# A two-layer hybrid decoder: the final norm moved into the last loop, new places for the hooked parts, and 18 matmuls whose results nobody reads

## The chip, the cores and the metric

The kernel runs on one core of a Trainium2 chip. The metric is the device time in microseconds (us) from launch to end; the time before is the median of three runs. The profile is one execution of the same program, and its span is counted from the first to the last instruction.

## The reference

A trunk of two layers over 512 tokens of width 1024, in float32, and a final RMSNorm. Cut to what matters:

```python
for l in range(2):
    xn = rmsnorm(h, norm_mix_g[l])
    c_q, c_kv, k_r, u = split(xn @ w_in[l])
    a_out = mla_group(c_q, c_kv, k_r, ...)      # 8 heads, low-rank q and kv, causal softmax
    s_out = s5_group(u, ...)                    # 32 groups, 64 complex states each, scan over time, GLU
    h = h + concat(rmsnorm(a_out, attn_out_g[l]), rmsnorm(s_out, ssm_out_g[l])) @ w_out[l]
    h = h + memory_cross_attention(rmsnorm(h, norm_x_g[l]), rmsnorm(mem, mem_norm_g[l]), ...)   # 4 heads, 256 tokens
    h = h + swiglu(rmsnorm(h, norm_ffn_g[l]), w_gate[l], w_up[l], w_down[l])                    # inner width 2816
return rmsnorm(h, final_norm_g)
```

## The kernel before, in words

Activations lie transposed, features on the 128 partitions and the 512 tokens along the free dimension; h is eight tiles of 128 x 512 (`self.hs`). Every large matmul is done as three float32r matmuls: a value is split into a high part (ScalarE, a copy to float32r) and a low part (VectorE or POOL, value minus high part), and `mm3` (lines 216 to 223) adds high x high, high x low and low x high in PSUM. Weights come as 128 x 1024 blocks through SyncE's queue and are split by `load_w` (lines 206 to 214). Eviction is mostly a VectorE product with the norm's row R, or the residual add (line 969).

A norm (`rms`, line 289) multiplies the sum of squares with a column of ones on TensorE (line 298), forms mean plus eps on VectorE (line 301) and the power −0.5 on POOL (line 303). `row` (line 276) then turns that column into a row on all partitions: high and low part (lines 280, 281), two matmuls with the identity for each 128 tokens (line 285), and ScalarE copies the result to SBUF as R (line 306).

The mixing stage of a layer is written by hand as an interleaving. The latent attention runs over units u = 0 to 16 (`mla`; scores at lines 737 to 740, outputs at 760 to 778, the next head's projections in `mla_qk` with the eviction at line 720). At each unit, hooked parts are issued as `PLAN[l]` lists them, as (unit, letter, index): `p` the S5 parameters of layer 0 (products at lines 573 and 509; tables written to DRAM as dBT, dCA and dQ), `v` the S5 input matmuls (line 820), `c` the scan, `m` and `y` the S5 outputs (lines 867 and 882), `G` and `g` the gated unit, `x` the memory's keys and values (blocks of 256 columns; `x` 4 to 7 are lines 961 to 965), `s` the S5 norm. Units below 0 are places before the attention. Layer 1's parameters are spread over layer 0's FFN by `FPLAN`, whose numbers are positions in that FFN (0 to 21 the inner blocks, from 22 the w_down blocks).

What sets the order of the work: the planner puts every engine's instructions in one list, by a priority number and by its own estimates of when an operand is ready; each engine then runs its list strictly in order. The priority number counts up in program order, and `later(off)` (line 197) shifts it for what is issued inside: `OFFS` for the hooked parts by letter, `P_OFF` for the parameters' TensorE steps, `PR_UP` and `MS_UP` for the start of layer 0. The constants that end in `POOL` say which steps go to POOL and which to VectorE. PSUM has eight buffers: mm 2, f 1, s 3, t 2.

`mix_out` (line 1001) starts w_out's S5 half (`mix_w`, lines 996 to 998) before the attention norm is through, for as many blocks as PSUM and the weight buffers hold, and adds the attention half (lines 1010 to 1012) behind it. In the last FFN, the last two of the eight w_down blocks (`TAIL = 2`) run over two halves of 256 tokens (line 1132 is their add); behind the loop, `final` (line 1134) takes the sum of squares, statistics, row and products (line 1149) of each half, and SyncE sends the output in eight transfers (line 1151).

## Time and profile before

| | us |
|---|---|
| median of three runs | 1598.01 (1595.21 to 1603.22) |
| the profiled execution, its own time | 1595.71 |
| its span, first to last instruction | 1593.9 |
| TensorE (PE) busy | 1519.3 (95%) |
| VectorE (DVE) busy | 908.6 (57%) |
| ScalarE (ACT) busy | 627.0 (39%) |
| POOL busy | 169.7 (11%) |
| TensorE's mean granted clock | 0.970 |
| HBM read and written | 152.10 MB and 17.76 MB |

The engines run beside each other, so their shares don't add up. A granted clock of 1.00 is 2.4 GHz, one of 0.50 is 1.2 GHz; a value between is a mean over a stretch. In the timeline, a row is a group of like instructions in time order: start, length, engine, line, operation, written tile <- read tiles, shapes and count; in brackets the idle time of that engine just before and what ended it. PEld, the weight loads, lies beside PE.

### The profile page before, as it was taken

How to read it: one execution, taken by the hardware profiler on the slowest of the kernel's cores; microseconds unless marked ns; L12 is line 12 of the kernel's file. 1: busy time of each engine (PE TensorE's matmuls, PEld its weight loads, DVE VectorE, ACT ScalarE, POOL GpSimd, SP SyncE). 2: the span in 40 equal slices, each digit the busy share in tenths (PEclk: the TensorE clock that was granted, in tenths of full speed). 3: DMA queues.
4: the chain of work that ended last, by engine and by line, in shares of the span. 5: the costliest groups of instructions: out<-in, count | busy, mean ns of one | idle time of the engine just before them, and what ended most of it. 6: DMA issues, size and time to landing. Idle time of an engine off the chain costs nothing.

```text
span 1593.9 us, 20203 instructions
## 1 busy us (share of the span) xinstructions
PE 1519.3 (95%) x8038; PEld 1258.6 (79%) x8038; DVE 908.6 (57%) x1274; ACT 627.0 (39%) x1027; POOL 169.7 (11%) x123
## 2 busy tenths in 40 slices
PE   7977999999999999999999899999999999999997
PEld 6766877887877888888886788778887888888886
DVE  7997546657685535435444954465655443543554
ACT  5543475444342322223333456644434222222333
POOL 4300001111131101101100100101000100110110
PEclk9987998999999999999999899999999999999998
DMA  6646633211352332232338454422122223223231
GB/s 222 156 139 152 131 121 119 94 67 53 126 146 93 112 106 93 87 112 93 109 132 158 127 143 124 138 74 93 40 79 94 79 93 106 93 87 112 93 92 62
DMA packets 93278, 173.27 MB, mean 109 GB/s; under 512 B 16512, under 2 KB 49792, under 8 KB 93184
## 3 DMA queue, kind: packets, MB, share of 16 engines
q1 hardware_dynamic: 93184, 171.99, 36.3%
q8 instruction: 63, 1.03, 0.3%
q14 instruction: 31, 0.25, 0.1%
HBM read 152.10 MB, written 17.76 MB: 107 GB/s over the span
## 4 chain that ended last, share of the span: by engine, by line
PE 83%; DVE 6%; DMA 4%; ACT 4%; issue 1%; SPq 1%; POOL 0%; DVEq 0%; ACTq 0%; POOLq 0%
PE mm L220 14%; PE mm L222 13%; PE mm L221 13%; PE f L220 7%; PE f L222 7%; PE f L221 7%; PE mm L768 2%; DVE lo L243 1%; PE t L760 1%; DVE wlo L214 1%; DMA s5b<-dQ 1%; ACT whi L213 1%; PE f L961 1%; PE f L962 1%; PE f L963 1%
## 5 line engine op out<-in xcount | busy, mean ns | idle before, releaser
L213 ACT ACTIVATE whi<-wraw 128x1024 fp32r<-128x1024 f32 (+1 forms) x234 | 243.6, 1043 | 643.8 <-PE mm L221 290.4
L214 DVE TENSOR_TENSOR wlo<-wraw,whi 128x1024 fp32r<-128x1024 f32 (+1 forms) x227 | 312.6, 1378 | 99.0 <-ACT whi L213 96.5
L220 PE MATMUL mm<-hi,whi 128*128 128x512 f32 x580 | 227.3, 392 | 0.5 <-ACT whi L213 0.5
L221 PE MATMUL mm<-lo,whi 128*128 128x512 f32 x580 | 225.8, 390 | 0.0
L222 PE MATMUL mm<-hi,wlo 128*128 128x512 f32 x580 | 225.7, 390 | 0.0
L220 PE MATMUL mm<-ghi,whi 128*128 128x512 f32 (+1 forms) x352 | 138.3, 393 | 1.6 <-DVE tmp L1108 0.8
L222 PE MATMUL mm<-ghi,wlo 128*128 128x512 f32 (+1 forms) x352 | 138.7, 394 | 0.0
L221 PE MATMUL mm<-glo,whi 128*128 128x512 f32 (+1 forms) x352 | 137.8, 391 | 0.2 <-DVE glo L243 0.2
L220 PEld LDWEIGHTS mm<-hi,whi 128*128 128x128 f32 x580 | 109.0, 188 | 26.0 <-ACT whi L213 2.8
L222 PEld LDWEIGHTS mm<-hi,wlo 128*128 128x128 f32 x580 | 108.8, 188 | 23.3 <-DVE wlo L214 0.4
L221 PEld LDWEIGHTS mm<-lo,whi 128*128 128x128 f32 x580 | 108.9, 188 | 22.4
L1114 POOL TENSOR_TENSOR tmp<-tmp,tmp 128x512 f32<-128x512 f32 x44 | 62.2, 1413 | 567.2 <-DVE tmp L1113 520.1
L220 PE MATMUL f<-ghi,whi 128*128 128x512 f32 (+1 forms) x304 | 107.0, 352 | 8.1 <-DVE s5b L950 2.4
L220 PE MATMUL f<-hi,whi 128*128 128x512 f32 x286 | 112.7, 394 | 1.6 <-DVE glo L243 1.4
L222 PE MATMUL f<-hi,wlo 128*128 128x512 f32 x286 | 111.9, 391 | 0.4 <-DVE wlo L214 0.4
L221 PE MATMUL f<-lo,whi 128*128 128x512 f32 x286 | 111.8, 391 | 0.0
L221 PE MATMUL f<-glo,whi 128*128 128x512 f32 (+1 forms) x304 | 106.6, 351 | 0.2 <-DVE glo L243 0.2
L222 PE MATMUL f<-ghi,wlo 128*128 128x512 f32 (+1 forms) x304 | 106.5, 350 | 0.3 <-DVE wlo L214 0.3
L969 DVE TENSOR_TENSOR s5b<-mm,s5b 128x512 f32<-128x512 f32 x53 | 36.6, 691 | 115.9 <-PE mm L222 96.7
L242 ACT ACTIVATE hi<-tmp 128x512 fp32r<-128x512 f32 (+1 forms) x100 | 62.5, 629 | 91.7 <-POOL tmp L1114 63.8
L220 PEld LDWEIGHTS mm<-ghi,whi 128*128 128x128 f32 (+1 forms) x352 | 66.0, 187 | 16.5 <-DVE tmp L1108 1.0
L222 PEld LDWEIGHTS mm<-ghi,wlo 128*128 128x128 f32 (+1 forms) x352 | 66.1, 188 | 14.8 <-DVE tmp L1108 0.3
(330 smaller groups left out, 2821.8 us busy)
## 6 DMA issues: line engine op xcount, KB each, us to landing
wraw<-w_gate SPq DMA_DIRECT2D x44, 512.0 KB, 3.3
wraw<-w_up SPq DMA_DIRECT2D x44, 512.0 KB, 3.3
wraw<-w_down SPq DMA_DIRECT2D x30, 448.0 KB, 3.3
wraw<-w_xkv SPq DMA_DIRECT2D x16, 512.0 KB, 4.0
wraw<-w_xv SPq DMA_DIRECT2D x16, 512.0 KB, 3.5
wraw<-w_out SPq DMA_DIRECT2D x16, 512.0 KB, 3.3
wraw<-w_xq SPq DMA_DIRECT2D x16, 512.0 KB, 3.3
wraw<-w_xo SPq DMA_DIRECT2D x16, 512.0 KB, 3.3
```

What stands on the lines that cost most here:

```text
L213: nc.scalar.activation(hi, raw, AF.Copy)
L214: (eng or nc.vector).tensor_tensor(lo, raw, hi.bitcast(F32), ALU.subtract)
L220: self.nc.tensor.matmul(ps, wh, xh, start=i == 0, stop=False)
L221: self.nc.tensor.matmul(ps, wh, xl, start=False, stop=False)
L222: last = self.nc.tensor.matmul(ps, wl, xh, start=False, stop=i == n - 1)
L242: a = nc.scalar.activation(hi, src, AF.Copy)
L243: b = eng.tensor_tensor(lo, src, hi.bitcast(F32), ALU.subtract)
L760: nc.tensor.transpose(pt[:, x * 128:(x + 1) * 128], p[ii][:, kb * 128:(kb + 1) * 128], self.ident)
L768: nc.tensor.matmul(po[64 * x:64 * x + 64, cs], vs[kb][:, (2 * pair + x) * 64:(2 * pair + x + 1) * 64], PT[x][:, kk * 256:min(n, kk * 256 + ...
L961: nc.tensor.matmul(o, xh[:, ts], wh[:, ks], start=hf == tb == k == 0, stop=False)
L969: self.nc.vector.tensor_tensor(self.hs[m], ps, self.hs[m], ALU.add)
L1114: nc.gpsimd.tensor_tensor(uf, uf, gf, ALU.mult)
```

## The change

Four things are changed; the arithmetic of the layers is not.

- The final norm moves into the loop over the two halves. `tail_start` squares and scales the first six blocks; `tail_end(cs)` does the last two, the statistics and the row of one half, right behind that half's matmuls. The row is made by one float32 matmul for each 128 tokens, without the split. The products of the first half are issued in the second half's `tail_end` and ordered behind its statistics on VectorE; those of the second half are five on VectorE, which read the row from PSUM, and three on POOL.
- `PLAN`, `OFFS`, `P_OFF`, `FPLAN`, `PR_UP` and `MS_UP` get other numbers.
- Steps move from POOL to VectorE: the memory statistics' adds (`MST_POOL`), four of layer 1's parameter products, of three steps each (`POOLQ`), and low parts of three projection weights (`IN_POOL`).
- `warm` issues matmuls of the identity with itself into a PSUM tile that the next real matmul starts afresh. Of its sites, three have a count in `WARM`: r13 and r15 (rows number 13 and 15 of the program, which are the attention norm and the FFN norm of layer 1) and w12 (the third w_out block of layer 1), six matmuls of 512 columns each.

`PSB` and `R_UP` repeat the values that held before.

```diff
@@ -139,23 +139,24 @@
...
+        self.BUFS = dict(self.BUFS, **dict(zip(("mm", "f", "s", "t"), self.PSB)))
-        self.n = self.np = 0
+        self.n = self.np = self.nrow = 0
...
     XKV_POOL = ()
-    GLU_POOL, MG_POOL, QK_POOL, ROPE_POOL, MST_POOL = 1, 0, 0, 0, 1
-    POOLQ = ((), (1, 3))
-    P_OFF = (500, 3000)
+    GLU_POOL, MG_POOL, QK_POOL, ROPE_POOL, MST_POOL = 1, 0, 0, 0, 0
+    POOLQ = ((), ())
+    P_OFF = (2850, 4550)
     SQ_PARTS, XLO_POOL = (0, 2, 4), ()
-    IN_POOL = ((2, 5), (3, 6))
+    IN_POOL = ((1, 3), ())
     KE_POOL, GL_POOL = ((0, 2), (0, 2)), ((), ())
     MN_POOL, MW_POOL = ((), ()), ((), ())
     YT, GT = "f", "t"
 
 
     PLAN = ((
-        (-4, "p", 0), (-4, "p", 1), (-4, "p", 2), (-4, "p", 3), (-4, "p", 4), (-1, "x", 0), (-1, "p", 5),
-        (-1, "x", 1), (-1, "x", 2), (1, "p", 6), (1, "p", 7), (1, "p", 8), (1, "p", 9), (1, "v", 0), (2, "m", 0),
-        (2, "m", 1), (2, "x", 3), (3, "m", 2), (3, "m", 3), (3, "x", 4), (4, "c", 0), (4, "c", 1), (8, "y", 0),
-        (10, "y", 1), (11, "y", 2), (11, "y", 3), (13, "G", 0), (13, "g", 0), (14, "x", 5), (14, "g", 1),
-        (14, "x", 6), (14, "g", 2), (15, "g", 3), (16, "x", 7), (16, "s", 0),
+        (-4, "p", 0), (-2, "p", 1), (-2, "p", 2), (-2, "p", 3), (-2, "p", 4), (-1, "x", 0), (-1, "x", 1),
+        (-1, "x", 2), (0, "p", 5), (1, "p", 6), (1, "p", 7), (1, "p", 8), (1, "p", 9), (1, "v", 0), (1, "m", 0),
+        (2, "m", 1), (2, "x", 3), (2, "m", 2), (3, "m", 3), (3, "c", 0), (3, "x", 4), (4, "c", 1), (5, "y", 0),
+        (9, "y", 1), (10, "y", 2), (10, "y", 3), (13, "G", 0), (13, "g", 0), (14, "g", 1), (14, "g", 2),
+        (15, "x", 5), (15, "x", 6), (15, "g", 3), (15, "x", 7), (16, "s", 0),
     ), (
-        (-2, "v", 0), (-2, "m", 0), (-1, "m", 1), (-1, "x", 0), (-1, "x", 1), (0, "c", 0), (0, "c", 1), (0, "x", 2),
-        (0, "x", 3), (0, "y", 0), (2, "m", 2), (4, "y", 1), (4, "y", 2), (8, "m", 3), (8, "y", 3), (9, "x", 4),
-        (10, "x", 5), (10, "G", 0), (13, "g", 0), (14, "g", 1), (14, "g", 2), (15, "g", 3), (16, "x", 6),
-        (16, "s", 0), (16, "x", 7),
+        (-2, "m", 0), (-2, "v", 0), (-2, "c", 0), (-1, "m", 1), (-1, "x", 0), (-1, "c", 1), (-1, "x", 1),
+        (0, "x", 2), (1, "y", 0), (3, "x", 3), (3, "m", 2), (4, "y", 1), (6, "y", 2), (6, "m", 3), (9, "y", 3),
+        (10, "x", 4), (10, "G", 0), (12, "x", 5), (14, "g", 0), (14, "g", 1), (14, "g", 2), (14, "g", 3),
+        (16, "x", 6), (16, "s", 0), (16, "x", 7),
     ))
-    OFFS = ({"x": 150, "m": 400, "s": 200, "c": 150, "G": 100, "v": 700, "g": 100, "y": -250, "p": 100},
-            {"y": -700, "c": 250, "v": 50, "g": 800, "m": 850, "G": 1300, "p": 100, "x": -100, "s": -50})
-    FPLAN = (0, 0, 1, 1, 1, 1, 1, 1, 2, 5)
-    PR_UP, MS_UP = 1500, 2300
+    OFFS = ({"x": 250, "m": 450, "s": -150, "c": 300, "G": -500, "v": 600, "g": -150, "y": -150, "p": 450},
+            {"y": -1300, "c": -300, "g": 250, "m": 1800, "G": 1550, "x": -100, "s": -300})
+    R_UP = 0
+    WARM = {"r13": 6, "w12": 6, "r15": 6}
+    PSB = (2, 1, 3, 2)
+    FPLAN = (2, 5, 6, 6, 13, 17, 19, 23, 29, 33)
+    PR_UP, MS_UP = 2000, 1400
 
     def t(self, shape, tag, dtype=F32, name=None):
         self.n += 1
...
+    def warm(self, site, ps):
+
+        n = self.WARM.get(site, 0)
+        w = ps.shape[-1]
+        rhs = self.identr if w < 512 else self.identr.unsqueeze(1).to_broadcast([128, 4, 128])
+        for _ in range(n):
+            self.nc.tensor.matmul(ps[:, :128] if w < 512 else ps, self.identr, rhs, start=True, stop=True)
 
...
         hi, lo = (self.t([128, 4], "cs", F32R)[:, :nb] for _ in range(2))
         nc.scalar.activation(hi, col, AF.Copy)
         nc.vector.tensor_tensor(lo, col, hi.bitcast(F32), ALU.subtract)
-        ps = self.p("t")[:, :nb * 128]
+        ps = self.p("t")
+        self.nrow += 1
+        self.warm(f"r{self.nrow}", ps)
+        ps = ps[:, :nb * 128]
         for b in range(nb):
             for x in (hi, lo):
                 nc.tensor.matmul(ps[:, b * 128:(b + 1) * 128], x[:, b:b + 1].to_broadcast([128, 128]), self.identr,
                                  start=x is hi, stop=x is lo)
         return ps
 
-    def rms(self, acc, dim):
+    def rms_col(self, acc, dim):
 
         nc = self.nc
         acc = acc if isinstance(acc, list) else [acc]
@@ -298,12 +313,18 @@
                 nc.tensor.matmul(ps[:, b:b + 1], x[:, b * 128:(b + 1) * 128], self.ones, start=i == 0,
                                  stop=i == len(acc) - 1)
         ms = self.t([128, 4], "stat")[:, :nb]
-        nc.vector.tensor_scalar(ms, ps[:, :nb], 1.0 / dim, EPS, ALU.mult, ALU.add)
+        self.stat_ins = nc.vector.tensor_scalar(ms, ps[:, :nb], 1.0 / dim, EPS, ALU.mult, ALU.add)
         col = self.t([128, 4], "stat")[:, :nb]
         nc.gpsimd.tensor_tensor(col, ms, self.mhalf[:, :nb], ALU.pow)
-        ps2 = self.row(col)
-        R = self.t([128, 512], "R")[:, :n]
-        nc.scalar.activation(R, ps2, AF.Copy)
+        return col
+
+    def rms(self, acc, dim):
+
+        with self.later(-self.R_UP):
+            col = self.rms_col(acc, dim)
+            ps = self.row(col)
+            R = self.t([128, 512], "R")[:, :ps.shape[-1]]
+            self.nc.scalar.activation(R, ps, AF.Copy)
         return col, R
 
 
...
+        self.warm(f"q{l}{hd}", ps)
+        self.warm(f"w{l}{m}", ps)
@@ -1122,6 +1151,7 @@
                 self.residual(ps, m, self.dh if last and l + 1 < self.depth else None)
                 hook(22 + 8 * ci + m)
             if nt:
+                self.tail_start()
                 ws = [self.load_w_slots(A[f"w_down{ci}"][l, m]) for m in range(KT - nt, KT)]
                 for cs in HALVES:
                     for m in range(KT - nt, KT):
@@ -1130,26 +1160,47 @@
                                        [y[:, cs] for y in Ys[k]]) for k in range(nk)])
                         h = self.hs[m][:, cs]
                         nc.vector.tensor_tensor(h, ps, h, ALU.add)
-
-    def final(self):
-        nc = self.nc
-        hs = self.hs
-        acc = None
-        n0 = KT - self.TAIL
-        for k in range(n0):
-            acc = self.square(acc, hs[k])
-            nc.scalar.activation(hs[k], hs[k], AF.Copy, scale=self.fin[:, k:k + 1])
-        for cs in HALVES:
-            for k in range(n0, KT):
-                self.square(acc[:, cs], hs[k][:, cs])
-                nc.scalar.activation(hs[k][:, cs], hs[k][:, cs], AF.Copy, scale=self.fin[:, k:k + 1])
-            _, R = self.rms(acc[:, cs], DM)
-            for k in range(KT):
-                h = hs[k][:, cs]
-                (nc.gpsimd if cs.start and k % 4 == 2 else nc.vector).tensor_tensor(h, h, R, ALU.mult)
-                if k % 2 == 1:
-                    nc.sync.dma_start(self.out[k - 1:k + 1, :, cs].rearrange("k p t -> p k t"),
-                                      self.hb[k // 4][:, k % 4 - 1:k % 4 + 1, cs])
+                    self.tail_end(cs)
+
+    def tail_start(self):
+
+        self.acc = None
+        for k in range(KT - self.TAIL):
+            self.acc = self.square(self.acc, self.hs[k])
+            self.nc.scalar.activation(self.hs[k], self.hs[k], AF.Copy, scale=self.fin[:, k:k + 1])
+
+    def tail_end(self, cs):
+
+        nc, hs = self.nc, self.hs
+        for k in range(KT - self.TAIL, KT):
+            self.square(self.acc[:, cs], hs[k][:, cs])
+            nc.scalar.activation(hs[k][:, cs], hs[k][:, cs], AF.Copy, scale=self.fin[:, k:k + 1])
+        col = self.rms_col([self.acc[:, cs]], DM)
+        if cs.start:
+            self.tail_scale(HALVES[0], self.tail_R, self.stat_ins)
+        ps = self.p("t")
+        self.warm(f"t{cs.start}", ps)
+        ps = ps[:, :256]
+        for b in range(2):
+            nc.tensor.matmul(ps[:, b * 128:(b + 1) * 128], col[:, b:b + 1].to_broadcast([128, 128]), self.ident,
+                             start=True, stop=True)
+        R = self.t([128, 512], "R")[:, :256]
+        nc.scalar.activation(R, ps, AF.Copy)
+        self.tail_R = (R, R)
+        if cs.start:
+            self.tail_scale(cs, (ps, R))
+
+    def tail_scale(self, cs, Rs, dep=None):
+        nc, hs = self.nc, self.hs
+        for k in range(KT):
+            h = hs[k][:, cs]
+            if k in (2, 4, 6) and cs.start:
+                nc.gpsimd.tensor_tensor(h, h, Rs[1], ALU.mult)
+            else:
+                self.after(nc.vector.tensor_tensor(h, h, Rs[0], ALU.mult), dep)
+            if k % 2 == 1:
+                nc.sync.dma_start(self.out[k - 1:k + 1, :, cs].rearrange("k p t -> p k t"),
+                                  self.hb[k // 4][:, k % 4 - 1:k % 4 + 1, cs])
 
     def part(self, f, i, off):
         with self.later(off):
@@ -1200,7 +1251,6 @@
                     if x == u:
                         self.part(params, i, 0)
             self.ffn(l, hook)
-        self.final()
 
 
 @with_exitstack
```

## Rows read from the trace of the kernel before

**Rows 1.** Which engine bounds: the page's busy times and its chain of work
```profile
PE 1519.3 (95%) x8038; PEld 1258.6 (79%) x8038; DVE 908.6 (57%) x1274; ACT 627.0 (39%) x1027; POOL 169.7 (11%) x123
...
PE 83%; DVE 6%; DMA 4%; ACT 4%; issue 1%; SPq 1%; POOL 0%; DVEq 0%; ACTq 0%; POOLq 0%
```

**Rows 2.** Table of stretches: start:end, length, busy (count) by engine, PEclk, DMA share, GB/s
```profile
60.00:80.00 20.00, 16.40 (x79) 13.15 (x77) 17.43 (x27) 15.43 (x27) 5.42 (x4) 0.83 0.56 156
...
80.00:100.00 20.00, 11.75 (x56) 9.61 (x57) 17.48 (x33) 10.90 (x26) 0.00 (x0) 0.74 0.36 119
...
120.00:140.00 20.00, 15.72 (x198) 13.93 (x197) 17.79 (x24) 6.50 (x11) 0.15 (x1) 0.76 0.83 237
...
140.00:160.00 20.00, 14.69 (x84) 12.61 (x84) 12.71 (x22) 7.35 (x18) 0.00 (x0) 0.73 0.56 66
...
260.00:280.00 20.00, 16.97 (x77) 13.55 (x74) 12.47 (x24) 7.60 (x15) 2.97 (x3) 0.66 0.22 77
...
560.00:580.00 20.00, 20.00 (x90) 16.57 (x89) 6.42 (x7) 4.09 (x4) 0.00 (x0) 1.00 0.32 106
...
880.00:900.00 20.00, 18.10 (x121) 14.56 (x117) 18.59 (x29) 10.61 (x18) 4.36 (x3) 0.66 0.38 127
...
1040.00:1060.00 20.00, 17.53 (x63) 13.07 (x64) 14.23 (x22) 9.37 (x16) 0.00 (x0) 0.83 0.08 26
```

**Rows 3.** Timeline of the tail: start, length, engine, line, operation [idle before <-releaser]
```profile
1579.05 0.50 PE L298 MATMUL t<-ones,tmp 128*128 128x1 f32 x4
...
1579.24 0.42 DVE L1132 TENSOR_TENSOR s5b<-f,s5b 128x256 f32<-128x256 f32 x1 [1.18 <-PE f L222]
...
1579.59 0.16 DVE L301 TENSOR_SCALAR stat<-t 128x2 f32<-128x2 f32 x1
...
1580.15 0.43 DVE L267 TENSOR_TENSOR tmp<-tmp,tmp 128x256 f32<-128x256 f32 x1 [0.40 <-ACT tmp L264]
...
1582.01 0.70 POOL L303 TENSOR_TENSOR stat<-stat,mhalf 128x2 f32<-128x2 f32 x1 [1.49 <-DVE stat L301]
...
1582.93 2.77 DVE L1149 TENSOR_TENSOR s5b<-s5b,R 128x256 f32<-128x256 f32 x8 [1.00 <-ACT R L306]
...
1585.62 0.15 DVE L281 TENSOR_TENSOR cs<-stat,cs 128x2 fp32r<-128x2 f32 x1
...
1585.83 0.90 PE L285 MATMUL t<-identr,cs 128*128 128x128 f32 x3 [2.31 <-DVE cs L281]
...
1587.18 3.15 DVE L1149 TENSOR_TENSOR s5b<-s5b,R 128x256 f32<-128x256 f32 x6 [1.41 <-ACT R L306]
...
1587.23 1.82 POOL L1149 TENSOR_TENSOR s5b<-s5b,R 128x256 f32<-128x256 f32 x2 [4.52 <-ACT R L306]
```

**Rows 4.** DMA view of 1575:1595, GB/s moved in 40 slices of 0.5 us
```profile
GB/s 0 0 0 0 0 0 0 16 0 0 0 0 0 0 0 0 0 0 0 213 338 326 344 354 344 178 0 0 63 344 240 334 334 352 350 80 0 0 0 0
```

**Rows 5.** Timeline of the attention norm of layer 1
```profile
1037.75 0.84 ACT L965 ACTIVATE s5b<-f,mcol 128x256 f32<-128x256 f32 x2 [1.36 <-PE f L963]
...
1039.48 0.60 ACT L306 ACTIVATE R<-t 128x512 f32<-128x512 f32 x1
...
1040.23 0.33 PE L285 MATMUL t<-identr,cs 128*128 128x128 f32 x1 [0.78 <-ACT cs L280]
...
1042.17 1.22 PE L996 MATMUL mm<-hi,whi 128*128 128x512 f32 x2 [1.62 <-ACT hi L242]
```

**Rows 6.** Timeline of PE at the FFN norm of layer 1
```profile
1232.70 0.53 PE L220 MATMUL f<-ghi,whi 128*128 128x512 f32 x1 [1.94 <-DVE tmp L1108]
```

**Rows 7.** Layer 0, PE's longest wait for a head; POOL's adds, grouped by form
```profile
84.27 0.79 PE L220 MATMUL mm<-hi,hi 128*128 128x512 f32 x1 [5.06 <-DVE tmp L720]
...
L394 POOL TENSOR_TENSOR tmps<-tmps,tmps 128x256 f32<-128x256 f32 x7 | 8.0, 1148 | 0.4
```

**Rows 8.** Layer 0, PE's wait for the S5 table; how long its reads take
```profile
149.98 3.65 PE L867 MATMUL f<-s5b,s5b 128*128 128x64 f32 x16 [5.32 <-issue]
...
DMA to landing us min/median/max: 3.3/7.1/9.2
```

More of the change, by code (lines that the diff above doesn't have):

```diff
@@ L877, in s5_y @@
         ps = self.p(self.YT)
+        self.warm(f"y{l}{q}", ps)
         for i in range(8):
@@ L945, in xkv @@
         ps = self.p("f")
+        self.warm(f"x{self.l}{i}", ps)
         if i < 4:
```

4 lines of the change are left out of this document (added).

## Prediction

> **What bounds the kernel now.** I read the page first: TensorE (PE) is busy 1519.3 of 1593.9 us, and the chain that ended last is 83% PE [rows 1]. The reader is to see that only two things can shorten such a run by much: time in which PE does nothing, and time in which it works at the lower of its two clock levels (a granted clock of 1.00 is 2.4 GHz, 0.50 is 1.2 GHz). So the next view was the table of 20 us stretches [rows 2]. Stretch 560:580, a plain one in the FFN, is what full use looks like: 20.00 us busy, clock 1.00, 90 matmuls of 512 columns or 0.222 us each. What a stretch loses against that is its idle time plus (1 − clock) × busy time. For 60:80 that is 3.6 + 0.17 × 16.4 = 6.4 us; for 80:100 11.3; 120:140 8.1; 140:160 9.3; 260:280 8.8; 880:900 8.1; 1040:1060 5.5. The same view shows the rest of 300 to 840 and of 1060 to 1560 nearly dense. So the losses lie where the hooked parts lie (the start of each layer and the two norms before w_out), and at the very end, where after the last matmul about 14 us are spent on the final norm. The third view was the timeline around each of these places.
>
> **The tail.** In the kernel before, the last matmul of w_down is done at about 1579.2, where DVE's add of it starts (1579.24); the row statistics of the first half start only there, at 1579.05, though that half of h is complete before the last 42 matmuls of 256 columns, some 5 us earlier [rows 3]. Then follow, one after another, the first half's statistics, its eight products (2.77 us, 0.346 each), the second half's row matmuls, held up because the DVE step that splits their input is queued behind those eight products (it runs at 1585.62), and the second half's products (1587.18 to 1590.34). The changed kernel puts the first half's statistics and row inside the loop, beside the second half's matmuls, drops the hi/lo split of the row, and lets the eight products of the first half run while the second half's POOL power and row matmuls run. Working: PE gets the first half's statistics (0.50 us) and row (two f32 matmuls of 128 columns, not in this form in the trace; bounded by the row of now, whose last three matmuls take 0.90 us, and a third of that) before its last matmul, so that one ends at 1579.2 + 1.0 = 1580.2. From there the second half goes through the residual add, square and accumulate (1579.24 to 1580.58, 1.34 us), the statistics (0.54 us from their start to the start of L301), and POOL (0.24 to its start, 0.70 long): its power is done at 1583.0, the row at about 1583.75. DVE meanwhile does the first half's eight products from 1582.3 to 1585.05, then five of the second half with R in PSUM (0.42 us each, by L1132, which also reads PSUM) to 1587.15; POOL does its three at 0.91 each from 1584.2 to 1586.95. The last product ends at 1587.2 instead of 1590.34: 3.1 us less. The eight output transfers then lie closer together. They move 2.1 MB at about 340 GB/s, 6.2 us, and now run in two bursts with a pause [rows 4]; from a first one at about 1583.9 they cannot end before 1590.1, against 1592.6 now, 2.5 us less. I take **−2.5 us**, between −1.5 (the row at its dearer end, and DVE and POOL slowing each other) and −3.1.
>
> That DVE and POOL slow each other is in the rows: with POOL beside it, DVE's six products take 3.15 us, 0.525 each, against 0.346 alone. The Trainium skill (SBUF — State Buffer, "Who interferes with whom") says that a DVE instruction with two SBUF inputs and a GpSimd instruction that reads SBUF exclude each other, and that one with at most one SBUF input does not. By that rule the first half's products that are left when POOL starts would wait for one POOL product, and the five with R in PSUM for none; the tail's gain would be some 0.9 us (one POOL product) smaller, 1.6 us. The 0.525 agrees for two SBUF inputs; no row shows a product with R in PSUM beside POOL.
>
> **The 18 unread matmuls.** Three groups of six with 512 columns: 6 × 0.222 = 1.3 us of PE at full clock and twice that, 2.7 us, at half clock [rows 2]. Sites r13 and w12 belong to the attention norm of layer 1. There PE waits 0.78 and 1.62 us between 1039.5 and 1042.2 [rows 5]; the clock of 0.83 over 1040:1060 is 0.17 × 20 / 0.5 = 6.8 us at half, to about 1048.8 [rows 2]. Nothing that w12 needs is missing in that gap (its PSUM buffer, read last by L965, is free at 1038.6), and r13 needs the other row buffer, which ACT has read by 1040.1 [rows 5]. Twelve matmuls are 2.7 us, and the gap less the one matmul in it is 2.4: cost 0.3 us. If the clock stays up, the 6.8 us of work at half take 3.4 us, 3.4 less; of that some 0.9 us may be lost again waiting for the low parts of the attention tiles. Net **−2.2 us**, between +2.7 (six at half clock on the path and no clock kept) and −3.0. Site r15 is the FFN norm of layer 1. There PE waits 1.94 us, but behind the row matmuls, for R and the first eviction [rows 6]. Six matmuls ahead of that row come while PE is dense: **+1.3 us**, between 0 (they fall in some gap) and +1.5. Both sites on PE's own queue hold up only what is behind them on PE.
>
> **The moved parts.** Nothing of the arithmetic changes, only the place of each part in the engines' queues, and which engine does some element work. (1) Layer 0's parameter parts p1 to p4 go from before the q and kv projections to after them, p5 a unit later, their PE steps later still (2850 for 500). At 84.27 PE waits 5.06 us for a DVE step of the first heads (L720) [rows 7]; DVE is busy 17.4 of 20 us in 60:80 and 17.5 in 80:100 [rows 2], a good part of it with parameter products (L573). Then the clock is at half for some 5 us. That stretch, 60 to 160, loses 35.1 us. If the parameter work is off the heads' way, a part comes back; the rest is the cost of getting DVE through its work at all. It also has a little more to do: seven adds of the memory statistics, 1.15 us each on POOL, at 0.43 us each on DVE (L267 at 256 columns) are 3.0 us, and the low part of one half-width weight some 0.7 us (a 512-column step at twice 0.346) [rows 3, 7]. I take **−5 us**, from −15 to +10: most of the wait of 5.06 and of the 5 us at half clock that follow it (2.5 lost), with the 3.7 us of extra DVE work set against part of it. (2) In layer 0 the S5 norm `s` gets its priority 350 steps earlier, and the last memory-value part x7 goes a unit earlier with its shift 100 later. Now x7 is done before the norms, and PE has nothing beside them: a clock of 0.66 over 260:280 and 3.0 us idle, 8.8 us lost [rows 2]. With x7 beside it, as layer 1 has it now, the loss is nearer layer 1's 5.5: **−3.3 us**, from −8 to +1. (3) In layer 1 `s` moves 250 earlier and the scan parts go ahead of the memory parts; 880:900 loses 8.1 us there, with DMA waits of the S5 input and half clock [rows 2]. **−2 us**, from −6 to +5. (4) Layer 1's parameters are spread over FFN units 2 to 33 instead of 0 to 5, and all on DVE: the four products moved from POOL are twelve steps of 512 columns, at twice 0.346 us some 8 us of DVE. They are hidden by PE, which is dense while DVE has 13.6 of 20 us free (560:580) [rows 2]; zero, and one or two us if an eviction waits behind one.
>
> **Sum.** 1593.9 − 2.5 − 2.2 + 1.3 − 5 − 3.3 − 2 = 1580.2 us of span. The profiled execution took 1595.7, 1.8 more than its span, so 1582.0; the median of the runs shown is 1598.0, 2.3 above it, so about **1584.3 us**, 0.9% less.
>
> **Rivals.** *A, the sum as above.* The chance is 0.52. *B, the moved parts balance out:* waits leave one place and turn up at another, since DVE's work at the start of layer 0 is no less and DVE is busy 87 to 89% in 60:80, 80:100 and 120:140 [rows 2]; only the tail and the three sites remain, −3.4 us, about 1594.6. For it speaks that PE waits in so many small places; against it that 260:280 is a plain hole. 0.23. *C, slower: the S5 chain comes last.* Layer 0's parameter parts write the tables dBT, dCA and dQ through DRAM; dQ is written at the end of the last part and read by the first `m` part, whose eight reads take up to 9.2 us to land. PE already stands 5.32 us before L867 at 149.98, most likely for that, since nothing else that the trace names ends this wait [rows 8]. Later parameters with `m` one unit earlier make this wait longer; it decides from the point where dQ is written more than some 5 us later against the heads than now. PE then stands once more as long as 120 to 160 loses now, 17.4 us, less the 8 us gained elsewhere: +9, about 1607. 0.12. *D, the front opens up:* the heads no longer wait for DVE, and of the 35.1 us in 60 to 160 some 17 come back instead of 5: about 1572. 0.13. That the unread matmuls don't stand where PE waits, so that the change there doesn't do what it says, is worth 12 × 0.222 + 2.2 = 5 us at most and is inside A's and B's width.
>
> **How the numbers follow.** A's own range is 1574 to 1594. A measurement of this kernel can tell about 0.5% from no change (the runs shown spread from 1595.2 to 1603.2), so faster is below 1590.0 and slower above 1606.0. A is below 1590 in nine cases of ten (0.47), D always (0.13), B one time in ten (0.02): faster 0.62. B's rest, A's tenth and a little of C: same 0.28. Slower 0.10. The range that leaves out 0.2 runs from 1568 to 1602.
>
> **What would show it.** Right: the last DVE product ends some 7 us after the last w_down matmul, not 11; the granted clock in the layer-1 attention norm stays at 1.00; 260:280 has a clock above 0.8; the wait for L720 in the first head is under 2 us. Wrong: PE's wait before L867 grows; six unread matmuls stand back to back in a dense stretch; new waits on DVE with L573 in front of L720 or L742; the eight outputs end later than 11 us after the last w_down matmul. The prediction fails as a whole if the losses between 60 and 160 don't fall, since they are half of all that can be gained.

## The result, and the profile after

The changed kernel takes 1576.35 us (median; 1572.02 to 1579.96) against 1597.53 beside it: ratio 0.9863, 95% interval 0.9846 to 0.9881, so 1.4% faster. The forecast was 1584.3, range 1568 to 1602, faster by over 0.5% at 0.62. Sign and range held; the forecast is 8 us too long, and two of its terms were wrong. The profiled execution is the longest of the four: 1579.96 us, span 1577.9. That matters below.

The page of the changed kernel, busy times and the chain that ended last (compare [rows 1]):

```profile
PE 1510.9 (96%) x8056; PEld 1249.6 (79%) x8056; DVE 909.6 (58%) x1293; ACT 625.2 (40%) x1025; POOL 134.9 (9%) x102
...
PE 82%; DVE 6%; ACT 5%; DMA 4%; issue 2%; SPq 1%; POOL 0%; POOLq 0%; ACTq 0%; DVEq 0%
```

PE still bounds. It is busy 8.4 us less although 18 matmuls were added, because it spends less time at the lower clock (mean granted clock 0.981 in this trace, 0.970 in the one before). The table of stretches of the changed kernel (columns as in [rows 2]):

```profile
60.00:80.00 20.00, 14.43 (x70) 10.37 (x68) 18.32 (x30) 12.98 (x24) 3.78 (x3) 0.91 0.46 145
80.00:100.00 20.00, 12.97 (x70) 10.60 (x71) 19.41 (x36) 12.94 (x28) 1.12 (x1) 0.86 0.38 124
120.00:140.00 20.00, 16.93 (x201) 14.30 (x201) 17.26 (x23) 8.52 (x16) 0.16 (x1) 1.00 0.79 234
140.00:160.00 20.00, 10.81 (x49) 9.02 (x49) 9.83 (x18) 5.74 (x15) 0.00 (x0) 0.55 0.58 59
260.00:280.00 20.00, 19.53 (x134) 17.81 (x135) 16.90 (x30) 12.63 (x22) 4.66 (x3) 1.00 0.40 134
880.00:900.00 20.00, 19.06 (x105) 15.77 (x106) 19.85 (x33) 15.73 (x29) 3.08 (x2) 0.84 0.53 159
1028.00:1048.00 20.00, 18.75 (x95) 14.97 (x94) 13.85 (x23) 10.18 (x17) 1.99 (x1) 1.00 0.08 27
```

The holes at 260:280 (clock 0.66 before, 1.00 now) and at the layer-1 attention norm (0.83 before; 1028:1048 now) are closed. In 60 to 160 the loss is 35.2 us, as before: 140:160 is worse, 120:140 better. 880:900 loses 4.0 where it lost 8.1.

A whole time scatters by some 8 us from run to run, so I cut each trace at instructions that every kernel has: layer 0's first cross score (line 1036 before, 1065 after), layer 1's first stats matmul, layer 1's first cross score, the stats of layer 1's FFN norm, the end of the span. Lengths in us between these points; each is the difference of two start times in the timeline (stats matmuls are the products with the column of ones):

| kernel | layer 0's mixing | rest of layer 0 | layer 1's mixing | cross | FFN and tail | median time |
|---|---|---|---|---|---|---|
| before | 342.7 | 485.1 | 287.4 | 106.1 | 372.6 | 1597.5 |
| changed | 342.6 | 485.7 | 275.7 | 106.1 | 367.7 | 1576.4 |
| after_again | 334.4 | 485.8 | 278.0 | 106.2 | 367.5 | 1575.5 |
| tail_only | 345.0 | 485.1 | 286.8 | 106.1 | 369.9 | 1594.2 |
| no_unread | 334.7 | 485.7 | 276.9 | 106.1 | 370.2 | 1576.8 |
| l0_old | 345.0 | 485.6 | 279.7 | 106.1 | 367.5 | 1584.6 |
| l1_old | 336.7 | 484.1 | 278.0 | 106.1 | 367.7 | 1575.2 |
| inproj_pool_old | 335.7 | 485.7 | 280.6 | 106.0 | 367.8 | 1579.8 |
| params_old | 336.0 | 483.7 | 279.1 | 106.1 | 367.3 | 1575.2 |
| layer1_old | 337.6 | 485.3 | 282.2 | 106.1 | 367.3 | 1579.9 |
| row_early | 337.7 | 484.2 | 277.2 | 106.1 | 365.7 | 1574.9 |
| x3_first | 341.0 | 484.0 | 277.5 | 106.1 | 367.6 | 1578.8 |
| skip_first | 333.1 | 485.8 | 278.0 | 106.1 | 367.5 | 1573.1 |
| both_fixed | 334.7 | 485.7 | 275.7 | 106.1 | 365.7 | 1571.7 |

In kernels that are alike there, cross and FFN repeat within 0.5 us, so differences of 1 us can be read there; the mixing stages, full of DMA waits, don't. From the first two rows alone layer 0 gained nothing and layer 1's mixing 11.7 us. The first half of that reading was wrong, as the next runs show. (The expectations of tail_only and l0_old read layer 0's score some 4.8 us later, at a later matmul of the same line: 347.4 or 347.5. The 1138.8 for layer 1 is likewise a later one.)

### The profile page after: what moved, and what is told of

It reads as the page before. It is cut to its first block, busy times and chain, and to the rows that moved or that the text cites. A ratio compares the mean times of both kernels' runs of the same rounds, so it can differ in the third digit from the quotient of the medians.

```text
span 1577.9 us, 20232 instructions
## 1 busy us (share of the span) xinstructions
PE 1510.9 (96%) x8056; PEld 1249.6 (79%) x8056; DVE 909.6 (58%) x1293; ACT 625.2 (40%) x1025; POOL 134.9 (9%) x102
## 4 chain that ended last, share of the span: by engine, by line
PE 82%; DVE 6%; ACT 5%; DMA 4%; issue 2%; SPq 1%; POOL 0%; POOLq 0%; ACTq 0%; DVEq 0%
PE mm L224 14%; PE mm L226 14%; PE mm L225 13%; PE f L224 8%; PE f L226 8%; PE f L225 8%; PE mm L790 2%; DVE lo L255 1%; DVE wlo L218 1%; PE t L782 1%; ACT hi L254 1%; ACT whi L217 1%; DMA s5b<-dQ 1%; PE f L891 1%; PE f L988 1%
## 5 line engine op out<-in xcount | busy, mean ns | idle before, releaser
L218 DVE TENSOR_TENSOR wlo<-wraw,whi 128x1024 fp32r<-128x1024 f32 (+1 forms) x230 | 315.9, 1374 | 90.3 <-ACT whi L217 87.7
```

The lines of the kernel that those rows point to most:

```text
L218: (eng or nc.vector).tensor_tensor(lo, raw, hi.bitcast(F32), ALU.subtract)
```

## The experiments

Each edit is against the changed kernel, if nothing else is said; where long lists are put back, only their names stand in it. A count at the end of a timeline row can stop at the edge of the window that was asked for.

### The yardstick, and layer 0

**after_again**: no edit. 

> The changed kernel once more, nothing altered, as the yardstick for the next two and as a second trace of it. Its first trace is the longest of its four runs, with the first layer-0 cross score at 342.6 us, while five kernels with the same layer 0 had it at 334.7 to 337.7. Theory: that first trace was the odd one; the score comes at 334 to 338 here and the time at 1575 to 1577. Rival: layer 0 falls on either of two lengths at random, as much on the long one; then 340 to 343 and the median nearer 1578.

The start of layer 0's first cross score, in the first and in this second trace of the changed kernel:

```profile
342.61 0.28 PE L1065 MATMUL s<-hi,hi 128*128 128x256 f32 x1
```
```profile
334.40 0.28 PE L1065 MATMUL s<-hi,hi 128*128 128x256 f32 x1
```

The same program, 8.2 us apart. The eight kernels with the changed layer 0 (changed, after_again, no_unread, l1_old, inproj_pool_old, params_old, layer1_old, row_early) lie at 334.4 to 342.6, mean 336.9; the one profiled first is the longest. In all eight, the instructions of layer 0 stand in the same order on PE, DVE, ACT and POOL, so none of their edits made this spread.

**l0_old**: layer 0 as before.

```diff
-    PLAN[0], OFFS[0]
+    PLAN[0], OFFS[0] of before
-    GLU_POOL, MG_POOL, QK_POOL, ROPE_POOL, MST_POOL = 1, 0, 0, 0, 0
+    GLU_POOL, MG_POOL, QK_POOL, ROPE_POOL, MST_POOL = 1, 0, 0, 0, 1
-    P_OFF = (2850, 4550)
+    P_OFF = (500, 4550)
-    IN_POOL = ((1, 3), ())
+    IN_POOL = ((2, 5), ())
-    PR_UP, MS_UP = 2000, 1400
+    PR_UP, MS_UP = 1500, 2300
```

> The changed kernel with layer 0's places put back as in the kernel before (plan and offsets of layer 0, when its parameter transposes are due, what GpSimd takes in the front); layer 1, the unread matmuls and the tail as in the changed kernel. It computes everything. Theory: layer 0's new places gave nothing (first layer-0 cross score at 347.4 in both traces; losses between 60 and 160 us 35.1 before, 35.2 after), so 1576.4 within 2 us, score at 347.5. Rival: the new places gave what they were costed at, 8.3 us, and something else in the changed kernel took as much away in layer 0; then putting them back leaves only the loss, and the score comes near 355, the whole near 1584.

Measured: 1584.59 us, ratio to before 0.9913 (0.9896 to 0.9930), apart from the changed kernel's interval; first score at 345.0. The theory, read from one trace, fell. Of the rival the price held, the new places are worth about 8 us, but not its reason: nothing else in the changed kernel took 8 us away in layer 0, its first trace was the long one. So the score came 2.3 us later than in that trace, not 7.6. The three traces with the old layer 0 have the score at 342.7, 345.0 and 345.0, mean 344.2, so 7.3 us.

### Layer 1: plan, weight splits, parameters

**l1_old**:

```diff
-    PLAN[1], OFFS[1]
+    PLAN[1], OFFS[1] of before
```

> The changed kernel with layer 1's places put back as in the kernel before (plan and offsets of layer 1 alone); layer 0, parameter steps beside the FFN of layer 0, the unread matmuls and the tail as in the changed kernel. It computes everything. Theory: of the 11.7 us that layer 1's mixing became shorter, 2.2 are the unread matmuls and about 9.5 are the places, in which the input projections' wait (2.99 us and half clock at 840 to 860 before) and that at 880 to 900 went: time 1585.9, ratio 0.993, layer-1 cross score 9.5 us later than in the changed kernel. Rival: the waits at 840 to 900 went because layer 1's parameter steps were taken from GpSimd and spread over the FFN of layer 0 (costed at nothing in the prediction); then they stay away here and the places are worth the 2 us they were costed at, 1578.4.

Measured: 278.0 us and 1575.24. The theory fell; the rival was right that the wait for u stays away, though not about its reason (params_old). Kernels with the new layer 1 have 275.7 to 278.0, mean 277.0 (after_again, row_early, x3_first, skip_first, both_fixed and the changed kernel), so the plan alone is worth about 1 us, no more than the scatter.

**inproj_pool_old**:

```diff
-    IN_POOL = ((1, 3), ())
+    IN_POOL = ((1, 3), (3, 6))
```

> The changed kernel with one thing put back: two of the eight weight splits of layer 1's input projections (the fourth and the seventh) on GpSimd again. In the order that comes of it the only other difference is that the first scan matmul of layer 1 stands 24 matmuls earlier again, ahead of the first q projection's block, as in the kernel before. It computes everything. From the first batch: with layer 1's old plan the stretch from layer 1's first stats matmul to its first cross score still took 278.0 us against 287.4 and 286.8 with everything of layer 1 old, so some 9 us do not hang on the plan. Theory: they hang on that split alone; the wait for the rearranged u (2.99 us) with the half clock behind it and what follows come back, the stretch rises from 275.7 to 276.9 to about 284 and the time from 1576.4 to about 1584. Rival: they hang on the parameter steps (next kernel); then the stretch stays within 2 us of 276 and only the wait of 3 us may show, made good later.

Measured: 280.6 us, 3.6 above the mean, and 1579.81 us. The timeline of this kernel, split, reads of u and first scan matmuls:

```profile
844.32 2.42 POOL L218 TENSOR_TENSOR wlo<-wraw,whi 128x1024 fp32r<-128x1024 f32 x1 [15.54 <-ACT whi L217]
...
842.32 3.64 SPq L656 DMA_DIRECT2D s5b<-du  x8
...
852.48 0.44 PE L843 MATMUL s<-s5b,raw 128*64 128x64 f32 x2 [2.35 <-DMA s5b<-dQ]
```

and of after_again:

```profile
841.14 3.64 SPq L656 DMA_DIRECT2D s5b<-du  x8
...
854.48 0.33 PE L843 MATMUL s<-s5b,raw 128*64 128x64 f32 x2
```

The slow split itself doesn't hold PE up: no wait for POOL shows in PE's rows of 820 to 900. But with it the planner's list has the first scan matmul 24 matmuls sooner, ahead of the block whose weight is split (that it expects this block later is my reading; that the place moves with this edit alone is in the lists). There the last reads of u have not landed: the last of them lands at 852.02 (the bracket names the reads behind them), PE waits 2.35 us, and the clock is 0.66 over 850 to 860. The four kernels with these two splits on POOL (before, tail_only, layer1_old and this one) all have the first scan matmul at that early place and a wait of 2.35 to 3.26 us there; in the other ten it stands 24 matmuls later and doesn't wait. The mechanism is the theory's, at half its size. The size rests on one trace, 2.6 us above the longest of the six; the intervals of the times overlap (ratio 0.9870 to 0.9909 against 0.9846 to 0.9881).

**params_old**:

```diff
-    POOLQ = ((), ())
-    P_OFF = (2850, 4550)
+    POOLQ = ((), (1, 3))
+    P_OFF = (2850, 3000)
...
-    FPLAN = (2, 5, 6, 6, 13, 17, 19, 23, 29, 33)
+    FPLAN = (0, 0, 1, 1, 1, 1, 1, 1, 2, 5)
```

> The changed kernel with layer 1's parameter steps put back as in the kernel before: all at the first blocks of layer 0's FFN, a quarter of their products on GpSimd, their transposes due sooner. The weight splits of layer 1's input projections stay on VectorE. It computes everything. Theory: nothing, as these steps end long before layer 1 begins: the stretch from layer 1's first stats matmul to its first cross score stays at 275.7 to 278, the FFN of layer 0 keeps its length (485.1 to 485.7 us from the first layer-0 cross score to layer 1's first stats matmul), time 1576.4. Rival: the steps' place is what shortened layer 1; then the stretch is near 284 here and the time near 1584.

Measured: 279.1 us, 1575.21. Two above the mean, but l0_old, which has the new parameter steps, has 279.7; the rival's 284 is far off. These two share one list of layer 1 (four matmuls of a projection stand six places later than in the changed kernel). No cost of the steps themselves shows.

**layer1_old**: the three edits together.

```diff
-    PLAN[1], OFFS[1], IN_POOL[1], FPLAN, POOLQ, P_OFF[1]
+    PLAN[1], OFFS[1], IN_POOL[1], FPLAN, POOLQ, P_OFF[1] of before
```

> The changed kernel with everything of layer 1's mixing put back: its plan and offsets, its parameter steps, and the two weight splits of its input projections on GpSimd. Layer 0, the unread matmuls and the tail are as changed. It computes everything. Measured alone against the sisters' 276.8 us from layer 1's first stats matmul to its first cross score: the plan 278.0, the parameter steps 279.1, the two splits 280.6, in sum 7.3 us; with all of it old and no unread matmuls 286.8 and 287.4. Theory: the three add up to within 2 us, and 283 to 286 is found, time about 1584. Rival: each is large only while the others are new, or two of them cover for each other; then it is over 286.5 or under 282.

Measured: 282.2 us, 5.2 above the mean, between the theory's sum and its rival. tail_only and before have 286.8 and 287.4; 1.4 of that is the unread matmuls (below). So some 3.5 us of layer 1's gain appear only with the new layer 0: layer1_old's list of layer 1 differs from before's in over 20 places, though its constants for layer 1 are the same. That the planner's estimates of layer 0 carry over into it is the likely reason, not a shown one, and which of the places does it was not tried.

### The unread matmuls

**no_unread**:

```diff
-    WARM = {"r13": 6, "w12": 6, "r15": 6}
+    WARM = {}
```

> The changed kernel without its 18 unread matmuls; nothing else differs, but the row matmuls of the layer-1 FFN norm fall back behind the third gate block, as in the kernel before. It computes everything. Theory: both waits come back. Layer-1 attention norm: a TensorE idle of some 1.6 us and a granted clock near one half in the 20 us around it, together +2.2 us at the first layer-1 cross score; FFN norm: the idle of about 1.9 us in front of the fourth block and half clock, +2.4 us at the FFN milestone behind it. Whole: +4.6 us over the changed kernel, 1581.0, ratio 0.9892. Rival: the gain at the FFN norm (2.4 us of the changed kernel against the one before) came from the layer-1 plan through buffers and not from the six matmuls there; then without them the stretch gets shorter by their 1.4 us, and the whole is +0.8 us, 1577.2.

Measured: 1576.75 us, where the theory wanted 4.6 more than the changed kernel; with runs of one kernel up to 8 us apart four runs don't settle that. The stretches do. FFN and tail: 370.2 against 367.3 to 367.8 in nine kernels with the unread matmuls and the row in its place, +2.5. Up to the tail's stats alone, 356.7 against 354.2 to 354.3. From the attention norm's stats to the first cross score: 82.04 against 80.65 in the changed kernel and 80.6 to 80.7 in eight others with layer 1's new plan, +1.4 (behind the gap, the planner also puts a few w_out matmuls elsewhere). The attention norm without them, and with them in the changed kernel:

```profile
1024.97 0.47 PE L300 MATMUL t<-identr,cs 128*128 128x128 f32 x1 [2.56 <-ACT cs L292]
1025.49 1.22 PE L1024 MATMUL mm<-hi,whi 128*128 128x512 f32 x2
```
```profile
1030.41 1.63 PE L246 MATMUL f<-identr 128*128 128x512 f32 x6
1031.88 1.54 PE L246 MATMUL t<-identr 128*128 128x512 f32 x6
1033.26 0.22 PE L300 MATMUL t<-identr,cs 128*128 128x128 f32 x1
```

The twelve fill a gap of 2.56 us and the matmuls behind them run at 0.22 and 0.39 us instead of 0.47 and 0.63; the clock over these 20 us is 0.83 without the twelve and 1.00 with them. The FFN norm without its six, and with them:

```profile
1203.47 0.95 PE L313 MATMUL t<-ones,tmp 128*128 128x1 f32 x8
...
1211.90 1.00 PE L300 MATMUL t<-identr,cs 128*128 128x128 f32 x8
...
1214.85 0.50 PE L224 MATMUL f<-ghi,whi 128*128 128x512 f32 x1 [1.94 <-DVE tmp L1137]
```
```profile
1210.19 0.95 PE L313 MATMUL t<-ones,tmp 128*128 128x1 f32 x8
...
1211.00 1.65 PE L246 MATMUL t<-identr 128*128 128x512 f32 x6
...
1213.79 0.16 DVE L293 TENSOR_TENSOR cs<-stat,cs 128x4 fp32r<-128x4 f32 x1 [1.42 <-ACT cs L292]
...
1218.17 1.00 PE L300 MATMUL t<-identr,cs 128*128 128x128 f32 x8
...
1219.84 0.69 DVE L1137 TENSOR_TENSOR tmp<-f,R 128x512 f32<-128x512 f32 x1 [3.00 <-ACT R L327]
```

Without them the wait of [rows 6] is back to the hundredth. With them the row comes 7.98 us behind the stats instead of 8.43 and, above all, with eight real matmuls fewer ahead of it: the six stand in for work that PE then still has while R is made. The clock over the second 10 us behind the stats is 0.83 without them and 1.00 with them.

**row_early**: no r15; the row put 18 matmuls behind the stats; two products of the tail freed.

```diff
-    WARM = {"r13": 6, "w12": 6, "r15": 6}
+    WARM = {"r13": 6, "w12": 6}
...
-    self.nc.tensor.matmul(ps, wh, xh, start=i == 0, stop=False)
+    self.after(self.nc.tensor.matmul(ps, wh, xh, start=i == 0, stop=False), self.row_ins if i == at else None)
...
-    self.mm_block(A["w_gate"][l, m], X, pg)
+    self.mm_block(A["w_gate"][l, m], X, pg, at=3 if (l, m) == (1, 1) else -1)
...
-    self.after(nc.vector.tensor_tensor(h, h, Rs[0], ALU.mult), dep)
+    self.after(nc.vector.tensor_tensor(h, h, Rs[0], ALU.mult), dep if k > 1 else None)
```

`row_ins` is the row's last matmul.

> The changed kernel without the six unread matmuls at the layer-1 FFN norm, but with the eight row matmuls of that norm put 18 matmuls behind its stats (they stand 31 behind them with the unread ones, 33 without), by an order between instructions of TensorE alone; and in the tail the first half's first two products no longer wait for the second half's stats. It computes everything. Two stretches are read apart. From the FFN norm's stats to the end: 367.7 us in the changed kernel, 370.2 without the unread matmuls. Theory: the row came too late for want of an early place, not for want of work; with the row some 3 us sooner the fourth block finds its PSUM free, no wait comes back without the unread matmuls, and their 1.4 us are saved too: 366.3; the tail, where the output transfers run without a gap to the end, ends another 0.9 sooner because they begin 0.9 sooner: 365.4 in all, time 1574.1. Rival: the unread matmuls are needed to hold the clock; then an idle of over 1 us or a granted clock under 1 shows in the 20 us behind the stats and the stretch is about 369.

```profile
1205.09 0.94 PE L313 MATMUL t<-ones,tmp 128*128 128x1 f32 x8
...
1210.12 1.36 PE L300 MATMUL t<-identr,cs 128*128 128x128 f32 x8
...
1212.15 0.69 DVE L1137 TENSOR_TENSOR tmp<-f,R 128x512 f32<-128x512 f32 x1 [1.72 <-ACT R L327]
```

Measured: 365.7 us, theory 365.4. The first eviction comes 7.06 us behind the stats (9.65 with the six unread), no PE wait for an eviction is left in that norm, and the clock is 1.00 in each of the next three 10 us stretches. In the changed kernel the row had stood in line 4.2 us after its operand was ready (1213.95 to 1218.17; 3.1 us without the unread matmuls); the unread matmuls only covered that. The run has two edits, and the tail's first stats matmul parts them: ahead of it 353.3 us against 354.2 to 354.3 with the six unread and 356.7 without, behind it 12.4 against 13.1 to 13.6. So the early row is worth 3.5 us where the six were worth 2.5, and the freed products some 0.9.

### The tail

**tail_only**: the kernel before, with the new tail alone (the edit is against the kernel before).

```diff
+                self.tail_start()
...
+                    self.tail_end(cs)
...
-        self.final()
```

> The kernel before with only the new tail: final norm inside the last loop over halves, no unread matmuls, every hooked part at its old place. It computes everything. Theory: the tail is worth 2.5 us of span (the end lay 2.5 us nearer to the last milestone in the trace of the changed kernel) and nothing ahead of it moves, so the first layer-0 cross score stays at 347.5 us, the first layer-1 one at 1138.8, and the time is 1595.0 (median of before 1597.5 less 2.5), ratio 0.9984. Rival: the earlier squares and scalings of the first six slabs push ScalarE and VectorE work of the last w_down blocks back, and part of the gain is given back ahead of the tail: the last VectorE addition comes later than in the kernel before, measured from the last milestone before it, and the whole gains under 1.5 us.

Measured: ratio 0.9982 (0.9970 to 0.9994); FFN and tail 369.9 for 372.6, so 2.7 us; theory held. (Its layer 0 has before's list in every place, so the 345.0 there is scatter.) The tail of the changed kernel, and the GB/s of its last 20 us in slices of 0.5 us (compare [rows 3, 4]):

```profile
1566.16 0.42 DVE L1162 TENSOR_TENSOR s5b<-f,s5b 128x256 f32<-128x256 f32 x1 [1.01 <-PE f L226]
...
1568.33 2.76 DVE L1200 TENSOR_TENSOR s5b<-s5b,R 128x256 f32<-128x256 f32 x8
...
1569.15 5.53 SPq L1202 DMA_DIRECT2D outT<-s5b  x8
...
1569.35 1.22 PE L1185 MATMUL t<-const,stat 128*128 128x128 f32 x4 [1.14 <-POOL stat L318]
...
1571.03 1.75 DVE L1200 TENSOR_TENSOR s5b<-s5b,t 128x256 f32<-128x256 f32 x5
1571.07 2.09 POOL L1198 TENSOR_TENSOR s5b<-s5b,R 128x256 f32<-128x256 f32 x3 [1.77 <-ACT R L1188]
```
```profile
GB/s 0 0 0 0 0 0 0 0 0 0 0 0 0 0 0 0 0 0 0 0 0 0 0 0 289 334 338 326 344 348 328 352 338 334 348 342 182 8 0 0
```

The two bursts have become one without a gap; it ends the kernel.

### The readout's wait in layer 0

**x3_first**:

```diff
-        (1, "v", 0), (1, "m", 0), (2, "m", 1), (2, "x", 3), (2, "m", 2),
+        (1, "v", 0), (1, "x", 3), (1, "m", 0), (2, "m", 1), (2, "m", 2),
```

> The changed kernel with one swap in layer 0's plan: the fourth part of the memory keys and values (48 matmuls of 256 columns, about 5.9 us) stands ahead of the scan's readout steps, not between the second and the third. It computes everything. In three traces of the changed layer 0 TensorE waits 6.3 to 7.5 us for the table that the first readout step reads back from DRAM, and the granted clock is at one half for some 20 us around it. Theory: the chain that ends in the table (a VectorE addition, the write, the read back) does not hang on that part, so the readout's wait falls by its 5.9 us to 0.5 to 2 us, the half clock at 140 to 165 goes, and layer 0's first cross score comes at 328 to 334 instead of 334.7 to 342.6: time about 1569. Rival: two wide weight splits of the moved part now stand ahead of that addition on VectorE and ScalarE, the chain ends later by as much, the wait stays over 5 us, and the time is 1575 to 1580.

Measured: 1578.76 us, 341.0. The theory fell. The rival's numbers came, a wait over 5 us and a time in its range, but not for its reason: the addition doesn't come later (132.8, 133.6 in the changed kernel), yet PE waits 6.27 us at the first readout, and a second wait is new:

```profile
160.63 3.76 SPq L885 DMA_DIRECT2D s5b<-dQ  x8
...
171.87 1.51 PE L891 MATMUL f<-s5b,s5b 128*128 128x64 f32 x6 [4.92 <-DMA s5b<-dQ]
```

The second half of the table is read only then. In the changed kernel the moved part ran just there, from 166.9 on, and covered it. The edit also moved other instructions: the list of PE in layer 0 differs in nine places.

**skip_first**:

```diff
-    V.tensor_tensor(tab[:, x], co(u), fi(cs), ALU.mult)
+    self.after(V.tensor_tensor(tab[:, x], co(u), fi(cs), ALU.mult), dsk if l == 0 else None)
```

`dsk` is the last skip addition (line 572).

> The changed kernel with one order added on VectorE: the two wide products for the scan's rotation table (1.9 us each) stand behind the last addition of the skip term in layer 0's parameter steps, not ahead of it. It computes everything. In the trace of the changed kernel ScalarE has handed over at 129.2 us, yet the addition runs at 133.6, behind those two products and one weight split; then the write (133.9) and the read back (137.9 to 143.7 issued) follow, and the first readout step waits to 152.1 with TensorE idle for 7.5 us. Theory: the readout's wait is that chain and nothing else; the addition comes about 3.7 us sooner (one weight split still stands ahead), the wait falls from 6.3 to 7.5 to about 3 us, the first layer-0 cross score comes 3 to 5 us sooner than the 336 us of its five sisters, time about 1572.5. Rival: the readout's inputs from the scan or the read of the first rows are as late; then the rotation table, now later by 1 us, makes the scan later and the wait stays over 5 us: 1575 to 1578.

The chain in the changed kernel:

```profile
128.81 3.76 DVE L586 TENSOR_TENSOR s5b<-s5b 128x1024 f32<-128x1024 f32 x2 [0.54 <-PE s L565]
...
133.63 0.23 DVE L572 SCALAR_TENSOR_TENSOR s5b<-const,gn,s5b 128x16 f32<-128x16 f32 x1
133.93 0.37 SPq L573 DMA_DIRECT2D dQ<-s5b  x1
137.93 0.81 SPq L885 DMA_DIRECT2D s5b<-dQ  x2
...
152.11 2.37 PE L891 MATMUL f<-s5b,s5b 128*128 128x64 f32 x10 [7.54 <-DMA s5b<-dQ]
```

and in skip_first:

```profile
128.50 0.23 DVE L572 SCALAR_TENSOR_TENSOR s5b<-const,gn,s5b 128x16 f32<-128x16 f32 x1
128.65 3.76 DVE L586 TENSOR_TENSOR s5b<-s5b 128x1024 f32<-128x1024 f32 x2
129.41 1.38 SPq L573 DMA_DIRECT2D dQ<-s5b  x1
133.70 5.70 SPq L885 DMA_DIRECT2D s5b<-dQ  x8
...
145.86 1.51 PE L891 MATMUL f<-s5b,s5b 128*128 128x64 f32 x6 [4.61 <-DMA raw<-w_uq]
```

The addition is 5 us sooner, the readout 6; but after_again, unaltered, has its readout at 146.4 with a wait of 4.6. The landing times show what ends the wait: in all fourteen traces the readout begins 0.2 to 0.5 us behind the landing of the last of the eight reads (151.87 in the changed kernel, 146.18 in after_again, 145.37 in skip_first). But that landing keeps no fixed distance from the addition: from its start to the readout pass 15.1 to 18.5 us in the eight kernels with one list of layer 0, 17.4 here (where the edit also changes PE's list of layer 0 in 13 places). Measured: 1573.06 us, ratio 0.9848 (0.9831 to 0.9866) beside 0.9863 (0.9845 to 0.9881) for after_again: inconclusive.

**both_fixed**: row_early and skip_first together.

```diff
+    the edits of row_early
+    the edit of skip_first
```

> The changed kernel with what the runs pointed to: the skip term's addition ahead of the rotation table's products in layer 0, the row matmuls of layer 1's FFN norm 18 matmuls behind its stats in place of six unread matmuls there, and the first two products of the final norm's first half not waiting for the second half's stats. It computes everything. Theory: the stretch from the FFN norm's stats to the end keeps the 365.7 us that it had in the run of the second and third of these (367.7 in the changed kernel), and the first is worth 3 to 5 us: 1576.4 - 2.0 - 3.5 = 1570.9. Rival: the first is worth nothing, and 1574.4.

Measured: 1571.70 us, ratio to before 0.9841 (0.9823 to 0.9859). Its FFN and tail keep the 2.0 us (365.7). For skip_first's edit the rival fits better: layer 0's mixing takes 334.7 us, as in after_again (334.4). The reads were issued 2.4 us sooner than there, but the first took 10.8 us to land instead of 5.3, and the last landed 1.0 later. The 3.8 us on after_again's 1575.54 are the best median of all, but the two intervals overlap, and in the traces 2.3 of it are layer 1's mixing, within its scatter.

## Why the prediction was right or wrong

**The tail**: −2.5 forecast, 2.7 measured, by the steps forecast: 7 us from the last addition to the last product (1566.16 to 1573.16), and transfers that close up and then set the end. The dearer price that the Trainium skill's rule gave (SBUF — State Buffer, "Who interferes with whom"; gain 1.6) did not come in the changed kernel's trace, but by luck: the matmuls of the second half's row ran at half clock (1.22 us), the row came late, and the first half's products end where POOL's start (1571.09 and 1571.07). In tail_only the same matmuls take 0.71 us, and POOL starts beside them:

```profile
1583.52 3.29 DVE L1200 TENSOR_TENSOR s5b<-s5b,R 128x256 f32<-128x256 f32 x8
...
1585.75 2.33 POOL L1198 TENSOR_TENSOR s5b<-s5b,R 128x256 f32<-128x256 f32 x3 [1.26 <-ACT R L1188]
```

There the eight products with two SBUF inputs take 3.29 us instead of 2.76 (the same in no_unread, l0_old and inproj_pool_old), as the rule says of them. The price at the end is small: the last product ends 7.1 us behind the last addition instead of 7.0. What the rule says of a product with one SBUF input agrees too: the five with R in PSUM took 0.35 us each beside POOL, not the 0.525 of two SBUF inputs [rows 3].

**r13 and w12**: −2.2 forecast, 1.4 measured; mechanism and place as forecast, clock 1.00, the size too large.

**r15**: +1.3 forecast, a gain of 2.5 measured. The step that failed is "six matmuls ahead of that row come while PE is dense", taken as a full cost. They do come there and take 1.65 us. But behind them stands a wait that was in my rows [rows 6]: PE runs out of PSUM before R comes. What is done ahead of such a wait is free up to its length, and the half clock behind it goes too. I had asked what the matmuls hold up, not what PE would do next.

**Layer 0, (1) and (2)**: −8.3 forecast, 7.3 by the traces, 8 by the times. The loss in 60 to 160 fell from 35.0 to 36.1 (three traces) to 30.0 to 35.2 (eight, mean 32.3): 3.4 of the 5 forecast. In 180 to 300 it fell from a mean of 13.4 to 8.7: 4.7 for 3.3. The wait for L720 is gone (5.06 to 0.5), but parameter transposes now wait for VectorE instead, 6.1 to 8.4 us in 55 to 100. The waits of PE in 55 to 100 in the changed kernel (line, what it waited for, us, times, longest):

```profile
PE s L542 <- DVE s5b L530: 8.2, 4, 3.8
...
PE mm L224 <- DVE tmp L742: 0.5, 1, 0.5
```

So B's mechanism took part of (1) back.

**Layer 1, (3)**: −2 forecast for the plan, about 1 measured, within the scatter.

**(4)**: the failed step. The parameters were priced at zero, and near zero they are. But the same lines of the diff move two weight splits of layer 1's input projections from POOL to VectorE, and I gave them no term at all. They are worth some 3.6 us, through the order that the planner makes of them. I had read where PE waits for u, and not why the waiting matmul stands there. With 3.5 us more that appear only with layer 0's new places (how is open) this is where the missing 8 us lie: layer 1's mixing gave 10.4 (287.4 to the mean of 277.0) where 4.2 were forecast, and r15 3.8 more than forecast, against 1 less from layer 0. That the time fell inside the range is no proof of these terms: the range is 34 us wide.

**Rival C**: its wait is there (5.32 before, 4.2 to 7.6 in the eight kernels) and hangs on the reads of the table, as it supposed, but did not grow enough to decide. **Rival D**: its 1572 lies nearer to the measured time than the sum does, but its mechanism didn't come: of its 17 us in 60 to 160, 3.4 did. **The last sentence of the prediction**, that all fails if 60 to 160 doesn't fall, was wrong: those losses fell by a tenth and the time by 21 us. They are the largest losses, and not the ones that could be had.

## What to carry to other kernels

Price every constant that a diff touches, also those that move work off an engine with time to spare: where a planner makes the lists, a slower operand on a free engine can move another instruction in front of its data. Work put ahead of a wait is free up to the wait's length, so look for the next wait before charging it; and then look whether what is waited for could have been issued sooner, which here gave more than the filling did (3.5 us against 2.5). Compare stretches between fixed instructions over several traces before believing that a part gained nothing: one trace was 8 us off in layer 0.

## What was not expected of the hardware

One program's layer 0 took 334.4 to 342.6 us; the readout's matmuls, behind a table written to DRAM and read back, began at 146.4 in one trace and at 152.1 in another. The eight reads of that table took SyncE 5.7 us to issue in the changed kernel and 10.1 in both_fixed, where they began 5 us sooner and the first of them took 10.8 us to land, not 5.4:

```profile
132.68 10.09 SPq L885 DMA_DIRECT2D s5b<-dQ  x8
```

And the four row matmuls of the tail took 1.22 us in the changed kernel and 0.71 in row_early, behind the same idle time of 1.14 us: the granted clock was 0.50 over 1569 to 1571 in the one and 1.00 over 1563 to 1564 in the other.

```profile
1563.26 0.71 PE L1185 MATMUL t<-const,stat 128*128 128x128 f32 x4 [1.14 <-POOL stat L318]
```
